# Hybrid decoder step on one core: where the last block's down weights are loaded and split, and when the last two attention heads' merge weights are formed

## The chip, the cores and the metric

One core of a Trainium2 chip runs the whole step as one program. The metric is device time in microseconds (us): the median of three runs, and beside it one profiled execution, whose rows are the ones read here. The core has five engines with a queue each: PE (TensorE, with its weight loads shown as PEld), ACT (ScalarE), DVE (VectorE), POOL (GpSimd) and SP, which here only issues transfers. An engine takes its instructions strictly in program order (the kernel fixes that order itself), so an instruction that waits holds up all behind it on the same engine.

## What is computed

One layer for 2048 prompt positions and 32 sample rows (8 sequences of 4), model width 1024, all in float32:

```
z = rmsnorm(x, g) @ w_in                     # q | k | v | u | gate
o, lse = three dilated attention branches    # 8 heads of 64; (128,1) (512,4) (2048,16)
att = sum_b softmax_b(lse_b) * o_b           # per position and head
x = x + concat(att, u * gate(v)) @ w_out
h = rmsnorm(x, g2)
x = x + (silu(h @ w_gate) * (h @ w_up)) @ w_down     # hidden width 2816
y = rmsnorm(x, final_g)
```

The outputs are y for prompt and sample, the key and value windows, and the sample rows of the gate.

## The kernel before

Every float32 product is made of two rounded halves ("high" and "low") and three matmuls: high·high, high·low, low·high. The halves come from `split_sb` (L132): ACT rounds (L135), POOL subtracts (L138).

**Attention** is a list of items, 20 for each of the 8 heads, one item to a step. Work is entered in a plan with `at(step, phase, fn)`, and written out sorted by step and, in a step, by the phase order `early, exp, low, scores, turn, mid, values, out, misc, store`. One item's scores are made in its step (PE L856, or L935 for the strided branch), its bias in the next (DVE L862 or L940), its exponential in the one after that (ACT L867 or L950), its transposes after that (PE L883 or L959), its values later (PE L911, L971). When a head is done, `Stats` (L987) forms the weights that merge its branches, in six parts entered by `stats_of` (L1142): `a` multiplies the collected maxima and sums by a mask (POOL L997, or DVE for the last head's second half), `b` is two small matmuls on it (PE L1003), `c` takes differences (DVE L1010 to L1013), `weights_e` exponentials (ACT L1016), `weights_b` the normalised weights (DVE L1021 to L1025), `store` writes them to DRAM (SP L1031). `merge_load` reads them back (SP L1045), `merge` applies them (L1054, L1056, L1058, on POOL or DVE), `merge_store` writes the merged head (SP L1063). Between the last head's steps ACT and POOL also split the first rows of w_out (tile v, loaded by SP L1313), and SP loads merged heads (L1350).

**The feed-forward part** runs in three blocks of tokens; the last one has four tiles of 128 prompt rows and the sample rows. A block goes through 22 slices f of the hidden width. For a slice, `one(u, q)` is called for q = 0 to 6: `product` (L1596) makes 12 matmuls (L1606 to L1608, 272 columns wide in the last block) from weights that ACT rounded (`high`, L1545) and POOL completed (`low_half`, L1549) during the slice before; then `prepare` (L1570) does the low half q-1 and the high half q of slice f+1 and loads piece q of slice f+2 (SP L1504, 256 KB); then perhaps one 512 KB piece of the sample cache is copied through (`roll`, SP L1258, at q = 1 and 3 in the last block); then the down weights. ACT also makes the silu (L1646, at q = 2 and 5) and the rounded hidden values (L1656, after q = 6); DVE makes their low halves (L1274).

The down weights of a slice are 512 KB. There is one raw buffer, fd: `load_down` (SP L1588) fills it and can only start when the split of the slice before has been read out; `split_down` makes the two halves (tile dw, ACT L135 and POOL L138). The down products (`down_unit`, L1679) are done for two slices at a time: at an even f, behind products 3, 4 and 5, for slices f-2 and f-1: two tiles of 24 matmuls, then two more, then the sample rows (8 matmuls). Each group of six takes three matmuls on the even slice's dw and hidden values, then three on the odd slice's. The last two slices are done after the loop by `first_downs` (L1683) and `last_rows` (L1728).

"e" is an even slice below, "o" the odd one behind it, and "o+1" the even one behind that, in which their down products run.

Of the kernel before, what the change touches and what calls it, by code (L numbers as in the profile page):

```python
# [28 lines left out]
NF = FF // P  # L29
# [13 lines left out]
class Plan:  # L43
# [8 lines left out]
    def at(self, step, phase, fn, *args):  # L52
        self.events.append((step, self.PHASES.index(phase), self.n, fn, args))
        self.n += 1
# [10 lines left out]
def hymba_step(ctx: ExitStack, tc: tile.TileContext, A: dict, O: dict):  # L65
    nc = tc.nc
    sync, act, dve, pool, pe = nc.sync, nc.scalar, nc.vector, nc.gpsimd, nc.tensor
# [7 lines left out]
    turn = [0, 0, 0, 0]  # L75
# [56 lines left out]
    def split_sb(hi, lo, src, eng_hi=None, eng_lo=None):  # L132

        if eng_hi is None:
            act.activation(hi, src, AF.Copy)  # L135
        else:
            eng_hi.tensor_copy(hi, src)
        (eng_lo or pool).tensor_sub(lo, src, hi.bitcast(F32))  # L138
# [22 lines left out]
    at = plan.at  # L161
# [517 lines left out]
    for half in range(2):  # L679
        for ki, kind in enumerate(ORDER[half]):  # L680
            for gi, tiles in enumerate(GROUPS):
# [13 lines left out]
                for j, tj in enumerate(tiles):  # L695
                    t = half * 8 + tj
                    e, ph = e0 + 2 * j, "out"
                    if last:
                        e, ph = e0, "early"
                    elif third:  # L700

                        e, ph = (e0 + 2 * j + 2, "out") if j < 2 else (e0, "early")
# [18 lines left out]
                    else:  # L721
                        layer_norm(e + 1, t, lambda t=t: zn["g", t], P, lambda t=t: gate_tile(t))

                        f = e + 4 + ((3 if half else 5) if tj in (4, 5) else 0)
# [417 lines left out]
    def stats_of(h, steps, r0, r1):  # L1142
        d = {}
        at(*steps[0], lambda: d.update(s=Stats(h, sts[h], r0, r1, dve if r0 else pool)))
        for (y, ph), fn in zip(steps, "a b c weights_e weights_b store".split()):
            at(y, ph, lambda fn=fn: getattr(d["s"], fn)())

    for h in range(H):

        s0 = B0 + (h + 1) * NI  # L1150
        end = h == H - 1
        ahead = h == H - 2
        if end:

            x = s0 - NI
            stats_of(h, [(x + y, ph) for y, ph in ((14, "early"), (14, "turn"), (15, "early"), (16, "early"), (16, "early"), (16, "mid"))], 0, 64)
            steps = ((2, "early"), (2, "turn"), (3, "early"), (4, "early"), (5, "early"), (5, "early"))
            at(x + 18, "mid", merge_load, h, 0)
            for part in range(3):
                at(x + 20 + part, "store", merge, h, 0, dve, part)  # L1160
                at(x + 21 + part, "store", merge, h, 1, pool, part)
            at(x + 24, "store", merge_store, h, 0, 2)
        else:
            steps = ((2, "misc"), (3, "misc"), (4, "early"), (5, "early"), (5, "misc"), (6, "mid"))

            for ch, (a, b) in enumerate(((8, 11), (8, 14), (11, 17), (11, 24) if ahead else (11, 20))):
                if ch % 2 == 0:
                    at(s0 + a, "mid", merge_load, h, ch)
                for part in range(3):
                    at(s0 + b + part, "store", merge, h, ch, pool, part)  # L1170
            if ahead:
                at(s0 + 17, "store", merge_store, h, 0, 2)
                at(s0 + 27, "store", merge_store, h, 2, 4)
            else:
                at(s0 + 23, "store", merge_store, h, 0, 4)
        stats_of(h, [(s0 + y, ph) for y, ph in steps], 64 if end else 0, P)
    for i, it in enumerate(items):
        x, h, n = B0 + i, it["h"], it["n"]
# [66 lines left out]
    def ob_pair(name):  # L1245
        t_ = lo.tile([P, 2, 1024], F32R, name=name, tag="ob", bufs=2)
        return t_[:, 0], t_[:, 1]
# [338 lines left out]
    def load_down(f):  # L1586
        raws["d", f] = w_ = pool_["fd"]
        sync.dma_start(w_, A["w_down"][f * P:(f + 1) * P, :])  # L1588
# [3 lines left out]
    def split_down(f):  # L1592
        wd[f % FC] = ob_pair("dw")
        split_sb(*wd[f % FC], raws.pop(("d", f)))
# [207 lines left out]
    B = blocks[0]  # L1802
# [55 lines left out]
    h = H - 1  # L1858
# [51 lines left out]
    def first_block(B):  # L1910

        m2, m1 = acc_place(2), acc_place(4)
        split_early(B, 1, m1)
        split_early(B, 2, m2)
        B.place()
        load_cat(B, 0, KD - 1, KD)
        load_cat(B, 5, 0, KD)
        merge_load(h, 2)
        load_acc(B, 1)
        load_acc(B, 0)  # L1920
        half1_load(*range(KD))
        sync.dma_start(gain[0], dap(A["final_g"], 0, [[0, P], [1, D]]))
        plan.run(10 ** 9)
        split_early(B, 3)
        for n, what in ((2, [(merge, h, 2, pool), (merge, h, 3, pool), (split_cat, B, 0), (split_early, B, 4)]),
                        (4, [(merge_store, h, 2, 4)]), (5, [(open_end, B, 1)]),
                        (6, [(half1_split, B, 0, 1)]), (7, [(open_end, B, 0), (split_cat, B, 5)]),
                        (8, [(half1_split, B, 2, 3)]), (9, [(half1_split, B, 4, 5), (sources, B, 0, 0, 1, 2, 3)]),
                        (10, [(half1_split, B, 6, 7)]), (11, [(sources, B, 1, 0, 1, 2, 3)])):
            later(n, both, *what)  # L1930
        for i in (1, 2, 3):
            open_unit(B, i)
        open_part(B, 0, (KD - 1,), False, True)
        for i in (4, 5):
            open_unit(B, i)
        first_operands(B)

        p2 = second_unit(B, 2)
        for i in (2, 3):
            load_acc(B, i)  # L1940
        second_end(B, 0, second_unit(B, 0))
        open_end(B, 2)
        second_end(B, 2, p2, 3)
        p1 = second_unit(B, 1)
        for i in (4, 5):
            load_acc(B, i)
        second_end(B, 1, p1)
        p3 = second_unit(B, 3)
        open_end(B, 3)
        second_end(B, 3, p3)  # L1950
        for i in (4, 5):
            open_end(B, i)
        for i in (4, 5):
            second_end(B, i, second_unit(B, i), 1)
# [54 lines left out]
    for bi, B in enumerate(blocks):  # L2009
        if bi == 0:  # L2010
            first_block(B)
        else:
            next_block(B, downs, finals)
        if B.last:
            hs4 = consts.tile([P, 4, 2 * SR], F32R, name="hs4", tag="cats")
        nb = None if B.last else blocks[bi + 1]

        part = 4
        units = [dict(f=f, a=0, b=B.nt) for f in range(NF)]
        if not B.last:  # L2020
            units[0:1] = [dict(f=0, a=0, b=part), dict(f=0, a=part, b=B.nt)]
        rows = list(range(len(B.rows)))
        last_h = {}

        def one(u, q):
            tick()
            product(B, u, q)
            f = u["f"]
            if u["b"] < B.nt:
                if bi == 0 and q in (0, 2):  # L2030
                    sources(B, 2, q, q + 1)
                return

            if f and q < 2:
                prepare(B, f, 7 + q)
            if f + 1 < NF:
                prepare(B, f + 1, q)
            if f + 2 < NF:
                if bi == 0 and f:
                    if q in (0, 2):  # L2040
                        sources(B, f + 2, q, q + 1)
                if bi == 0:
                    ahead_of(f + 2, q)
            elif nb:

                for s in {(0, 2): (0, 1), (0, 4): (2, 3), (1, 3): (4, 5), (1, 5): (6, 7)}.get((f + 2 - NF, q), ()):
                    load_wo(0, s, fraw)
                if f + 1 == NF and q > 0:
                    split_wo(nb, 0, q - 1, lambda s: op_tile())
            if f + 1 < NF and q in (1, 3, 5)[:(1, 3, 2)[bi]]:  # L2050
                roll(1)

            if q == 2 and f:
                load_down(f)
            elif q == (5 if f % 2 else 6):
                split_down(f)

        def downs_of(pair, a, b):
            for i in rows[a:b]:
                down_unit(B, i, pair)  # L2060

        for n, u in enumerate(units):
            u["n"] = n
            for q in range(7):
                one(u, q)
                if u["f"] % 2 == 0 and u["f"] > 0 and 3 <= q < 6:
                    downs_of((B.h[0], B.h[1]), *((0, 2), (2, 4), (4, 9))[q - 3])
        pair = (B.h[0], B.h[1])
        if B.last:
            last_rows(B, pair)  # L2070
        else:

            last = ([4] if nb.last else []) + [i for i in rows if not (nb.last and i == 4)]
            downs = [lambda B=B, pair=pair: first_downs(B, last[0], last[1], pair)]
            downs += [lambda B=B, pair=pair, i=i: down_unit(B, i, pair) for i in last[2:]]
            finals = [lambda B=B, nb=nb, i=i: final_a(B, i, (load_acc, nb, i) if i < len(nb.rows) else None) for i in last]
# [104 lines left out]
```

## Time and profile before

| | us |
|---|---|
| median of three runs | 2521.73 (2508.28, 2521.73, 2523.93) |
| profiled execution, its own time | 2527.26 |
| its span, first to last instruction | 2525.4 |
| PE busy in the span | 2442.6 (97%) |
| POOL, DVE, ACT busy | 1303.2, 1270.2, 1130.9 |
| mean granted TensorE clock | 0.989 |

A row of the timeline has start, length, engine, line, operation, output and inputs, and in brackets the idle time before it and who ended it. A row of the windows view has, for each engine, busy time and number of instructions in a stretch, then the granted clock and the transfers' share. SPq rows are transfers at their issue.

### The profile page before, as it was taken

The numbers are of one execution on the slowest core, as the hardware profiler recorded it, in microseconds if no ns is written. First come the engines' busy times: TensorE is split into PE (matmuls) and PEld (weight loads), VectorE is DVE, ScalarE is ACT, GpSimd is POOL, SyncE is SP. The second block draws the span as 40 slices with busy tenths as digits, with TensorE's granted clock in tenths as the row PEclk, the third lists the DMA queues.
The fourth block names the chain that finished last, engine by engine and source line by source line (L and its number), as shares of the span: only waits on it lengthen the run. The fifth ranks groups of instructions, "written<-read, shape, count | busy, mean of one in ns | idle before, by whom it ended". The sixth has DMA issues, their size and how long they took to land.

```text
span 2525.4 us, 39104 instructions
## 1 busy us (share of the span) xinstructions
PE 2442.6 (97%) x14022; PEld 2116.0 (84%) x14022; DVE 1270.2 (50%) x2595; ACT 1130.9 (45%) x2449; POOL 1303.2 (52%) x1019
## 2 busy tenths in 40 slices
PE   8998999999999899999999999999999998999997
PEld 7877776668887678999999989999999978888986
DVE  4558582217776645444444465444444465444444
ACT  7324343226666556454554446233233255333334
POOL 2216441005778447676776626445355445556565
PEclk9999999999999899999999999999999999999999
DMA  9974845675554554555555363535445363555553
GB/s 294 280 230 148 259 127 175 200 253 175 182 168 131 142 191 154 167 175 179 155 194 166 128 218 134 188 136 199 170 169 203 117 223 126 175 200 178 197 174 132
DMA packets 292292, 455.36 MB, mean 180 GB/s; under 512 B 28711, under 2 KB 160984, under 8 KB 286980
## 3 DMA queue, kind: packets, MB, share of 16 engines
q1 hardware_dynamic: 285252, 440.82, 53.6%
q10 hardware_dynamic: 6848, 12.06, 1.7%
q8 instruction: 111, 1.82, 0.3%
q14 instruction: 81, 0.66, 0.1%
HBM read 365.07 MB, written 157.84 MB: 207 GB/s over the span
## 4 chain that ended last, share of the span: by engine, by line
PE 62%; POOL 6%; issue 6%; DVE 3%; DMA 3%; ACT 2%; SPq 0%; POOLq 0%; DVEq 0%; ACTq 0%
PE ps_o L1679 15%; PE ps_m L1608 9%; PE ps_m L1607 9%; PE ps_m L1606 9%; POOL op L1549 4%; PE ps_s L856 3%; PE ps_o L911 2%; PE ps_t L883 1%; PE ps_s L935 1%; PE ps_s L318 1%; PE ps_o L1373 1%; PE ps_o L1375 1%; PE ps_o L1374 1%; PE ps_m L1373 1%; PE ps_m L1375 1%
## 5 line engine op out<-in xcount | busy, mean ns | idle before, releaser
L1549 POOL TENSOR_TENSOR op<-fr,op 128x512 fp32r<-128x512 f32 x385 | 487.5, 1299 | 246.6 <-ACT op L1545 232.5
L1606 PE MATMUL ps_m<-xh,op 128*128 128x384 f32 (+3 forms) x1904 | 604.9, 318 | 0.7 <-DVE zn L1627 0.4
L1608 PE MATMUL ps_m<-xh,op 128*128 128x384 f32 (+3 forms) x1904 | 604.4, 317 | 0.0
L1607 PE MATMUL ps_m<-xl,op 128*128 128x384 f32 (+3 forms) x1904 | 603.9, 317 | 0.1
L1679 PE MATMUL ps_o<-dw,hw 128*128 128x512 f32 x2040 | 492.6, 396 | 20.4 <-POOL dw L138 12.6
L1679 PEld LDWEIGHTS ps_o<-dw,hw 128*128 128x128 f32 x2040 | 385.1, 190 | 106.3 <-POOL dw L138 16.5
L1606 PEld LDWEIGHTS ps_m<-xh,op 128*128 128x128 f32 x1904 | 360.2, 189 | 5.3 <-ACT xh L1450 0.7
L1607 PEld LDWEIGHTS ps_m<-xl,op 128*128 128x128 f32 x1904 | 360.0, 189 | 4.0 <-DVE xl L1462 0.4
L1681 DVE TENSOR_TENSOR acc<-acc,ps_o 128x512 f32<-128x512 f32 (+1 forms) x362 | 248.3, 687 | 226.8 <-PE ps_o L1679 226.8
L1608 PEld LDWEIGHTS ps_m<-xh,op 128*128 128x128 f32 x1904 | 359.9, 189 | 0.0
L1646 ACT ACTIVATE ps_t<-zn 128x384 f32<-128x384 f32 (+1 forms) x126 | 58.5, 465 | 500.7 <-DVE zn L1629 423.8
L138 POOL TENSOR_TENSOR dw<-fd,dw 128x1024 fp32r<-128x1024 f32 x66 | 158.5, 2401 | 204.2 <-ACT dw L135 194.0
L1545 ACT ACTIVATE op<-fr 128x512 fp32r<-128x512 f32 x396 | 233.8, 626 | 3.4 <-PE ps_m L1375 3.4
L318 PE MATMUL ps_s<-wh,xh 128*128 128x512 f32 x480 | 196.8, 410 | 6.0 <-ACT xh L135 6.0
L320 PE MATMUL ps_s<-wh,xl 128*128 128x512 f32 x480 | 189.0, 394 | 0.0
L319 PE MATMUL ps_s<-wl,xh 128*128 128x512 f32 x480 | 188.9, 394 | 0.0
L1549 POOL TENSOR_TENSOR op<-pair,op 128x512 fp32r<-128x512 f32 x63 | 81.3, 1298 | 113.7 <-ACT op L1545 109.3
L536 POOL TENSOR_TENSOR pr<-kv,qb 96x512 f32<-96x512 f32 x32 | 45.6, 1425 | 170.3 <-DMA kv<-in_cache_k_dram 86.1
L318 PEld LDWEIGHTS ps_s<-wh,xh 128*128 128x128 f32 x480 | 90.9, 189 | 48.5 <-issue 23.7
L1656 ACT ACTIVATE hw<-ps_t 128x384 fp32r<-128x384 f32 (+1 forms) x126 | 54.2, 449 | 157.7 <-DVE ps_t L1652 157.7
L927 POOL CAST sq<-k 128x512 fp32r<-128x512 f32 x32 | 34.1, 1066 | 164.8 <-PE ps_s L319 164.8
L1274 DVE TENSOR_TENSOR hw<-ps_t,hw 128x384 fp32r<-128x384 f32 (+1 forms) x120 | 59.3, 508 | 109.7 <-ACT hs L1660 57.0
(490 smaller groups left out, 4328.7 us busy)
## 6 DMA issues: line engine op xcount, KB each, us to landing
fr<-ab_d SPq DMA_DIRECT2D x308, 256.0 KB
fd<-in_w_down_dram SPq DMA_DIRECT2D x66, 512.0 KB
out_ks_dram<-in_cache_k_dram SPq DMA_DIRECT2D x56, 512.0 KB
out_vs_dram<-in_cache_v_dram SPq DMA_DIRECT2D x56, 512.0 KB
ab_d<-fr SPq DMA_DIRECT2D x88, 256.0 KB
qk_d<-pair SPq DMA_DIRECT2D x64, 256.0 KB
ab_d<-pair SPq DMA_DIRECT2D x63, 256.0 KB
kv<-in_cache_k_dram SPq DMA_DIRECT2D x64, 192.0 KB
```

The source lines that it names most:

```text
L138: (eng_lo or pool).tensor_sub(lo, src, hi.bitcast(F32))
L318: pe.matmul(o[j], xh[:, k, :], wh, start=(k == 0), stop=False)
L319: pe.matmul(o[j], xh[:, k, :], wl, start=False, stop=False)
L320: pe.matmul(o[j], xl[:, k, :], wh, start=False, stop=(k == KD - 1))
L856: pe.matmul(s[:, a:b_], d[q][:, qs], d["k"][:, t0:t0 + b_ - a], start=(z == 0), stop=(z == 1))
L1545: act.activation(ops[f, j][0], ab[f][j], AF.Copy)
L1549: (pool if f or j in POOL_LOW else dve).tensor_sub(lo_, ab[f][j], hi.bitcast(F32))
L1606: pe.matmul(out, wh[:, ks], xh[:, :, k], start=(k == 0), stop=False)
L1607: pe.matmul(out, wh[:, ks], xl[:, :, k], start=False, stop=False)
L1608: pe.matmul(out, wl[:, ks], xh[:, :, k], start=False, stop=(k == 3))
L1679: pe.matmul(ps[0:nr], l_, r_[:, cs], start=(z == 0 and y == 0), stop=(z == FC - 1 and y == len(pairs) - 1))
L1681: dve.tensor_add(B.acc[i][0:nr, cs], B.acc[i][0:nr, cs], ps[0:nr])
```

## The change

Two things. In the last block, `split_down(f)` of an odd slice is called at q = 3 and not at q = 5, and `load_down(f + 1)` is called directly behind every split, where before `load_down(f)` stood at q = 2 of its own slice. In the other blocks nothing moves. In the attention, for the next to last head and the first half of the last one, the parts `b` to `store` of the merge weights are entered one step later (part `a` stays), and DVE's three parts of the last head's first merge one step later too.

```diff
-            stats_of(h, [(x + y, ph) for y, ph in ((14, "early"), (14, "turn"), (15, "early"), (16, "early"), (16, "early"), (16, "mid"))], 0, 64)
+            stats_of(h, [(x + y, ph) for y, ph in ((14, "early"), (15, "turn"), (16, "early"), (16, "early"), (17, "early"), (17, "mid"))], 0, 64)
...
-                at(x + 20 + part, "store", merge, h, 0, dve, part)
+                at(x + 21 + part, "store", merge, h, 0, dve, part)
...
-            steps = ((2, "misc"), (3, "misc"), (4, "early"), (5, "early"), (5, "misc"), (6, "mid"))
+            steps = (((2, "misc"), (4, "misc"), (5, "early"), (6, "early"), (6, "misc"), (7, "mid")) if ahead else
+                     ((2, "misc"), (3, "misc"), (4, "early"), (5, "early"), (5, "misc"), (6, "mid")))
...
-            if q == 2 and f:
+            if B.last:
+                if q == (3 if f % 2 else 6):
+                    split_down(f)
+                    if f + 1 < NF:
+                        load_down(f + 1)
+            elif q == 2 and f:
                 load_down(f)
             elif q == (5 if f % 2 else 6):
                 split_down(f)
```

(`ahead` is true for the next to last head.) In the changed program the lines from L1165 to L2052 carry a number one higher, so L1504 is L1505 there.

SP in the last block, one odd slice and the start of the even one (out<-in of each transfer; fr are pieces of the next slices' weights, out_vs the cache copies). Before:

```order
994 L1504 DMA fr<-ab_d 128x512
995 L1588 DMA fd<-in_w_down_dram 128x1024
996 L1504 DMA fr<-ab_d 128x512
997 L1258 DMA out_vs_dram<-in_cache_v_dram 16x8192
998 L1504 DMA fr<-ab_d 128x512 x5
999 L1258 DMA out_vs_dram<-in_cache_v_dram 16x8192
1000 L1504 DMA fr<-ab_d 128x512
```

and now:

```order
1002 L1505 DMA fr<-ab_d 128x512 x3
1003 L1589 DMA fd<-in_w_down_dram 128x1024
1004 L1505 DMA fr<-ab_d 128x512 x2
1005 L1259 DMA out_vs_dram<-in_cache_v_dram 16x8192
1006 L1505 DMA fr<-ab_d 128x512 x2
1007 L1259 DMA out_vs_dram<-in_cache_v_dram 16x8064
1008 L1589 DMA fd<-in_w_down_dram 128x1024
```

The odd slice's fd has moved ahead of two fr pieces, a cache copy and a third fr piece; the even slice's stands behind the cache copy of q = 3.

ACT around the split of an odd slice (op is a high half, the first L1646 the silu of q = 2, the second that of q = 5, hw and hs the hidden values). Before:

```order
1744 L1646 ACTIVATE ps_t_23656<-zn 128x272
1745 L1545 ACTIVATE op<-fr 128x512 x3
1746 L1646 ACTIVATE ps_t_23720<-zn 128x272
1747 L1545 ACTIVATE op<-fr 128x512
1748 L135 ACTIVATE dw<-fd 128x1024
1749 L1656 ACTIVATE hw<-ps_t_23720 128x4x64
```

and now:

```order
1751 L1647 ACTIVATE ps_t_23657<-zn 128x272
1752 L1546 ACTIVATE op<-fr 128x512 x2
1753 L135 ACTIVATE dw<-fd 128x1024
1754 L1546 ACTIVATE op<-fr 128x512
1755 L1647 ACTIVATE ps_t_23724<-zn 128x272
1756 L1546 ACTIVATE op<-fr 128x512
1757 L1657 ACTIVATE hw<-ps_t_23724 128x4x64
```

The split has moved ahead of two high halves and the second silu. On POOL it moves likewise: between the even and the odd split stand four low halves where six stood, and behind the odd split ten where eight stood.

PE in the last head, around the first half's two small matmuls (ps_o and ps_t with a number are banks of PSUM). Before:

```order
3062 L856 MATMUL ps_s<-k,ql 128x256
3063 L1003 MATMUL ps_o_8785<-sel_r,sm 64x16 x2
3064 L883 MATMUL ps_t_8788<-ident,e 128x128 x3
3065 L883 MATMUL ps_t_8793<-ident,e 128x128 x2
3066 L971 MATMUL ps_o_8796<-eT,v 64x64 x8
```

and now:

```order
3062 L856 MATMUL ps_s<-k,ql 128x256
3063 L883 MATMUL ps_o_8785<-ident,e 128x128 x3
3064 L883 MATMUL ps_t_8790<-ident,e 128x128 x2
3065 L971 MATMUL ps_o_8793<-eT,v 64x64 x8
3066 L856 MATMUL ps_s<-k,qh 128x384
3067 L856 MATMUL ps_s<-k,qh 128x256
3068 L856 MATMUL ps_s<-k,ql 128x384
3069 L856 MATMUL ps_s<-k,ql 128x256
3070 L1003 MATMUL ps_t_8817<-sel_r,sm 64x16 x2
```

The two matmuls have moved behind the transposes and strided values of their own step and the scores of the next. On DVE the parts `c` and `weights_b` each move behind one more pair of L894 (a transposed piece) and L862 (a bias). For the next to last head the two matmuls move behind only two score matmuls.

## The prediction

> **What bounds the kernel now.** First the page's busy times: PE works nearly all the time, so only what leaves PE standing or slows it can be gained.
>
> ```profile
> PE 2442.6 (97%) x14022; PEld 2116.0 (84%) x14022; DVE 1270.2 (50%) x2595; ACT 1130.9 (45%) x2449; POOL 1303.2 (52%) x1019
> ```
>
> Then the waits of PE in the stretch of the last block, and the first tile pair of each of its ten groups of down products, in the windows view (L1679 only; granted clock third from the right, of 1.00):
>
> ```profile
> PE ps_o L1679 <- POOL dw L138: 11.6, 10, 1.3
> PE ps_o L1679 <- ACT hw L1656: 4.5, 6, 1.2
> ...
> 2137.80:2149.10 11.30, 8.84 (x24) 6.28 (x24) 0.70 0.54 168
> 2177.50:2187.00 9.50, 7.63 (x24) 5.41 (x24) 0.82 0.56 176
> ...
> 2287.20:2296.40 9.20, 7.63 (x24) 5.43 (x24) 0.81 0.55 171
> 2324.80:2334.90 10.10, 7.55 (x24) 5.42 (x24) 0.83 0.56 169
> 2363.30:2369.60 6.30, 5.75 (x24) 4.29 (x24) 1.00 0.38 113
> ...
> sum 83.70, PE 67.10 PEld 48.27; mean PE 6.71 PEld 4.83
> ```
>
> The second pair of a group is the same 24 matmuls and waits for nothing:
>
> ```profile
> 2297.93 5.63 PE L1679 MATMUL ps_o<-dw,hw 128*128 128x512 f32 x24
> 2303.40 0.29 PE L1606 MATMUL ps_m<-xh,op 128*128 128x272 f32 x1
> ```
>
> It takes 2303.40 - 2297.93 = 5.47, 0.228 a matmul. Ten take 54.7; the first pairs take 83.7, from which 0.5 goes off because the stretches' edges are rounded outward. **So 28.5 us are lost there**, more than the 16.1 that the waits add up to. Four pairs ran at a lowered clock: 11.3 x 0.30 + 9.5 x 0.18 + 9.2 x 0.19 + 10.1 x 0.17 = 8.6. The other 19.9 is waiting, part of it hidden by modelled ends.
>
> One group shows why. Rows of PE, SP, ACT and POOL in turn:
>
> ```profile
> 2269.07 0.29 PE L1606 MATMUL ps_m<-xh,op 128*128 128x272 f32 x1
> 2285.72 0.29 PE L1606 MATMUL ps_m<-xh,op 128*128 128x272 f32 x1
> ...
> 2287.22 0.86 PE L1679 MATMUL ps_o<-dw,hw 128*128 128x512 f32 x3
> 2288.28 0.49 PE L1679 MATMUL ps_o<-dw,hw 128*128 128x512 f32 x1 [0.20 <-ACT hw L1656]
> 2290.12 6.45 PE L1679 MATMUL ps_o<-dw,hw 128*128 128x512 f32 x20 [1.35 <-POOL dw L138]
> ...
> 2279.03 0.52 SPq L1258 DMA_DIRECT2D out_vs_dram<-in_cache_v_dram  x1
> 2280.28 0.42 SPq L1588 DMA_DIRECT2D fd<-in_w_down_dram  x1
> ...
> 2272.59 1.06 ACT L135 ACTIVATE dw<-fd 128x1024 fp32r<-128x1024 f32 x1
> 2276.14 1.66 ACT L1545 ACTIVATE op<-fr 128x512 fp32r<-128x512 f32 x3
> 2286.55 1.06 ACT L135 ACTIVATE dw<-fd 128x1024 fp32r<-128x1024 f32 x1 [5.27 <-DMA fd<-in_w_down_dram]
> ...
> 2273.73 2.40 POOL L138 TENSOR_TENSOR dw<-fd,dw 128x1024 fp32r<-128x1024 f32 x1 [3.48 <-ACT dw L135]
> 2276.08 7.53 POOL L1549 TENSOR_TENSOR op<-fr,op 128x512 fp32r<-128x512 f32 x6
> 2287.69 2.38 POOL L138 TENSOR_TENSOR dw<-fd,dw 128x1024 fp32r<-128x1024 f32 x1 [4.07 <-ACT dw L135]
> ```
>
> PE starts product 6 of e at 2269.07 and is at product 3 of o+1 at 2285.72: eleven products in 16.65, 1.51 each. The odd fd is issued at 2280.28, 1.25 behind a cache copy of the same size, and lands at 2286.55, 6.3 later. ACT has stood 5.27 for it, with hw queued behind; POOL's low half begins at 2287.69, and the fifth matmul of the group, which reads it, at 2290.12 instead of 2287.22 + 4 x 0.228 = 2288.13.
>
> **Down weights, part by part.** Nothing is added: the same 21 loads and 22 splits, in other places.
>
> The load. fd is free when POOL has done the even split, 2273.73 + 2.40 = 2276.13. SP is then at this load; the next fr waits for POOL's next low half (2276.08 + 1.26) anyway, so no transfer behind it is held up. Issue: 2276.2, 4.1 earlier. How long it takes on a quiet queue the last slice shows, whose load found nothing before it:
>
> ```profile
> 2494.50 0.34 SPq L1588 DMA_DIRECT2D fd<-in_w_down_dram  x1
> 2498.66 0.40 ACT L1646 ACTIVATE ps_t<-zn 128x272 f32<-128x272 f32 x1 [4.12 <-DVE zn L1629]
> 2499.00 1.04 ACT L135 ACTIVATE dw<-fd 128x1024 fp32r<-128x1024 f32 x1
> ```
>
> ACT went from the silu into the split without a gap: at most 4.5. Behind a cache copy it took up to 7.2:
>
> ```profile
> 2317.92 0.43 SPq L1588 DMA_DIRECT2D fd<-in_w_down_dram  x1
> 2325.16 1.06 ACT L135 ACTIVATE dw<-fd 128x1024 fp32r<-128x1024 f32 x1 [6.23 <-DMA fd<-in_w_down_dram]
> ```
>
> Bounds for the landing are thus 4.5 and 7.2. I take 4.5: in the new order the copies of q = 1 stand behind the load.
>
> ACT. At q = 3 it has done two of three high halves, at 2276.14 + 1.11 = 2277.25, and waits for the landing at 2280.7; the split ends at 2281.8. Queued behind are a high half (1.66 / 3 = 0.55), the silu of q = 5 and hw: silu to 2282.7, DVE's product of it 0.45 (row below), hw and a second round by about 2284.4. PE wants hw of o as its fourth matmul, 2287.91. So 3.5 us cover it; DVE, which waits for the silu, holds a PSUM bank that PE needs at 2285.72, with 2 us to spare.
>
> ```profile
> 2280.76 0.45 DVE L1652 TENSOR_TENSOR ps_t<-ps_t,raw 128x272 f32<-128x272 f32 x1 [0.47 <-ACT ps_t L1646]
> ```
>
> POOL. Four low halves from 2276.08 end at 2281.1; the split runs from 2281.8 to 2284.2; **the next low half, that of q = 3, ends at 2285.45**. PE reads it as third matmul of product 3, at 2285.72 + 0.25 = 2285.97. Here is the thin cover, 0.5 us: a landing later than 5.0 makes PE wait here, microsecond for microsecond. The down products, from 2287.2, find both halves of dw done.
>
> The even load, issued near 2284.2 for a split near 2310, has some 25 us, and SP's fr pieces behind it wait for low halves that POOL does later still. In the last pair the load waits for the split of slice 20 as before; ACT now stands at q = 3 for it and makes the silu behind the split, some 1.4 later (one split, and a landing up to 0.3 behind where the silu was); the first twelve matmuls of the end, 12 x 0.228 = 2.7, still cover hw, barely. **Term: -28.5** (between -28.5 and, at 7.2, about +10; worked out under the rivals).
>
> What lowers the clock matters. LDWEIGHTS of L1679 shows two speeds, and each of the four lowered pairs holds waits of 2 us or less and no other cause that I see:
>
> ```profile
> L1679 PEld LDWEIGHTS ps_o<-dw,hw x2040: 186/188/334, 998.7 to 2513.8; 128*128 128x128 f32 x186
> ```
>
> The Trainium skill ("TensorE: Matmul & The Clock Gate", Part 1: The HAM clock gate) has the clock fall to half after an idle window of about 3.4 us. The near half speed agrees; the idle length does not, since no wait here is as long.
>
> **Merge weights.** Three places, rows of PE, ACT, DVE:
>
> ```profile
> 820.43 0.62 PE L1003 MATMUL ps_o<-sel_r,sm 128*128 128x16 f32 x4 [2.07 <-POOL sm L997]
> 843.77 0.61 PE L1003 MATMUL ps_o<-sel_r,sm 128*64 128x16 f32 x4 [2.19 <-POOL sm L997]
> 849.71 0.69 PE L911 MATMUL ps_o<-pt,v 128*64 128x256 f32 x2 [0.58 <-ACT o L981]
> 856.10 0.56 PE L856 MATMUL ps_s<-k,qh 128*128 128x384 f32 x2 [2.12 <-DVE st L862]
> 868.66 0.59 PE L1003 MATMUL ps_t<-sel_r,sm 128*128 128x16 f32 x4 [1.86 <-DVE sm L997]
> ...
> 848.75 0.63 ACT L135 ACTIVATE op<-v 128x512 fp32r<-128x512 f32 x1 [3.01 <-DMA v<-in_w_out_dram]
> ...
> 851.51 1.24 DVE L1021 TENSOR_TENSOR dd<-f,s 64x16 f32<-64x16 f32 x1 [4.67 <-ACT f L1016]
> 866.70 0.94 DVE L1056 TENSOR_TENSOR o<-o,raw 128x256 f32<-128x256 f32 x1
> ...
> 840.00:850.00 10.00, 7.24 (x58) 5.89 (x58) 2.97 (x12) 4.24 (x11) 4.18 (x6) 0.69 1.00 241
> ```
>
> At 820 the small matmuls pass two score matmuls (about 0.6); at 843.77 the wait of 2.19 is filled with transposes, values and scores. But PE's next stop, 849.71, waits for ACT, and ACT for a w_out piece until 848.75, with the transfers 1.00 busy. PE came to the wait at 843.77 - 2.19 = 841.58; the work behind it took 849.13 - 844.38 = 4.75, much of it at the lowered clock, and is now done by 846.3 or sooner. So PE only stands longer at 849.71, 3.4 or more: both gains are lost at this point. Behind it DVE's wait of 4.67 has one bias less queued, so the 2.12 at 856.10 can go; against it, the longer stand can cost a lowered stretch, up to 10 x (1 - 0.69) = 3.1. At 868.66 DVE's L997 now runs ahead of L1056: -0.8. The next to last head's weights, formed behind one more DVE pass (such as L1056's 0.9), can delay the transfers that PE meets at 849.71, since SP takes them in order. Bounds: -0.8 - 2.1 = -2.9 and 3.1 + 0.9 - 0.8 = +3.2. **Term: -1.0**, the certain 0.8 and a little of the 2.12.
>
> **Sum.** 2527.3 - 28.5 - 1.0 = 2497.8 against the profiled execution's own time. That execution is 5.5 above the median; if its lowered stretches are part of that, the gain at the median is up to 5.5 smaller. From 2521.7 this gives 2492.2 to 2497.7; I take 2495.0. A measurement of this kernel tells about 1% from no change, 25.2 us: below 2496.5 is faster.
>
> **The rivals.**
> (a) *POOL's low half takes the place.* The load still takes about 5.7, since fr pieces crowd it: 0.7 of wait in each of ten groups at product 3, and lowered stretches stay (8.6). Gain 28.5 + 1.0 - 7 - 8.6 = 14: 2508. For it: only 0.5 us of cover. Against: nothing is issued for 5.9 us before the load.
> (b) *The same place, slower.* At 7.2 each group waits 2.2 and draws a lowered stretch (8.6 / 4 = 2.15): 10 x 4.35 = 43.5 against 28.5, so +15, less 1: 2536. It decides from a landing of about 5.0 + 0.7 = 5.7 with such stretches, or 7.9 without. Against it: the same row order as in (a).
> (c) *The clock is not lowered by these waits* but by something that stays. Then 8.6 stays: 2495 + 8.6 = 2503.6. For it: six pairs with like waits kept 1.00. Against: the quoted second pair, the same matmuls without waits, ran at full speed. The Trainium skill's rule on idle windows, named above, would speak for this one.
> (d) *The change does not do what it says:* the load cannot leave earlier because fd is read until later. The rows give fd free at 2276.13, so only if POOL were behind. 2521.
>
> **How the numbers follow.** Forecast 0.70, (a) 0.12, (b) 0.05, (c) 0.09, (d) 0.04. The forecast's own spread, 2488 to 2501 from the merge term and the median, lies for about 0.7 of it below 2496.5: 0.49, and (a) and (c) add 0.01. Faster by over 1% 0.50, within 1% 0.46, slower 0.04, most of (b). Range 2486 to 2513: it takes in (a) and (c) and leaves out (b) and (d).
>
> **What would show it.** Right: in the last block L1679's waits for dw and hw gone, each first pair at 5.47, clock 1.00 there; ACT waiting 3 to 4 us for fd at q = 3, load to split start under 5 us; L1608 without waits for POOL. Wrong: L1608 waiting for POOL op L1549, or load times above 5.7. In the attention: no PE wait at 843, a longer one at 849, L1003's last wait about 1 us.

## The result and the profile after

| | before | after |
|---|---|---|
| median (lowest to highest), us | 2521.73 (2508.28 to 2524.78, 5 runs) | 2497.71 (2491.31 to 2498.77, 5 runs) |
| profiled execution, its own time | 2527.26 | 2497.73 |
| its span | 2525.4 | 2495.9 |
| granted clock, mean | 0.989 | 0.992 |

The ratio is 0.9898, with a 95% interval from 0.9867 to 0.9929: 24 us, or 1.0%, faster. The profiled executions differ by 29.5, more than the medians; where the other 5 come from is told below.

The page's busy times after, then all waits of PE in the stretch of the last block (2060 to the end):

```profile
PE 2430.9 (97%) x14022; PEld 2111.4 (85%) x14022; DVE 1273.4 (51%) x2595; ACT 1131.7 (45%) x2449; POOL 1305.1 (52%) x1019
```

```profile
PE ps_t L1440 <- ACT pair L1493: 3.5, 1, 3.5
PE ps_o L1680 <- DVE acc L1682: 1.5, 1, 1.5
PE ps_t L1440 <- ACT xns L1427: 1.1, 1, 1.1
PE ps_m L1607 <- ACT xh L1451: 0.5, 1, 0.5
```

No wait of the down products (L1680) for dw or hw is left, and none of the products (L1607 to L1609) for POOL has come. PE has as many matmuls as before and is busy 11.7 less: matmuls at a lowered clock, and the modelled ends of waiting ones, count as busy. The first tile pairs of the down products, in the windows view (L1680 only; clock third from the right):

```profile
2136.80:2142.40 5.60, 5.55 (x24) 4.37 (x24) 1.00 0.92 320
...
2442.30:2447.90 5.60, 5.53 (x24) 4.39 (x24) 1.00 0.94 330
sum 55.90, PE 55.42 PEld 43.68; mean PE 5.54 PEld 4.37
```

Each of the ten takes 5.49 from its first matmul to the product behind it, and has the full clock. By the same measure they took 83.2 before and 54.9 now: **28.3 us of the 29.5 come from here**.

One group after, SP, ACT, POOL and PE in turn:

```profile
2261.57 0.33 SPq L1589 DMA_DIRECT2D fd<-in_w_down_dram  x1
...
2265.03 1.06 ACT L135 ACTIVATE dw<-fd 128x1024 fp32r<-128x1024 f32 x1 [2.34 <-DMA fd<-in_w_down_dram]
...
2259.15 2.40 POOL L138 TENSOR_TENSOR dw<-fd,dw 128x1024 fp32r<-128x1024 f32 x1 [3.48 <-ACT dw L135]
2261.50 5.04 POOL L1550 TENSOR_TENSOR op<-fr,op 128x512 fp32r<-128x512 f32 x4
2266.48 2.42 POOL L138 TENSOR_TENSOR dw<-fd,dw 128x1024 fp32r<-128x1024 f32 x1
2268.83 5.08 POOL L1550 TENSOR_TENSOR op<-fr,op 128x512 fp32r<-128x512 f32 x4
...
2272.63 5.65 PE L1680 MATMUL ps_o<-dw,hw 128*128 128x512 f32 x24
```

The load leaves as POOL ends the even split (2259.15 + 2.40 = 2261.55), and ACT starts the odd split 3.46 later. POOL has both low halves of dw done at 2268.9, 3.7 before the down products begin. The low half of q = 3 is done at 2268.83 + 5.08 / 4 = 2270.10; PE reads it as third matmul of a product that begins 1.51 before the group, at 2271.37: 1.3 us of cover.

In the attention, rows of PE, one of ACT, and the windows view around the wait:

```profile
822.57 0.62 PE L1003 MATMUL ps_o<-sel_r,sm 128*128 128x16 f32 x4 [1.56 <-POOL sm L997]
845.26 0.41 PE L1003 MATMUL ps_t<-sel_r,sm 128*64 128x16 f32 x4 [0.28 <-POOL sm L997]
851.24 2.40 PE L911 MATMUL ps_o<-pt,v 128*64 128x256 f32 x12 [4.88 <-ACT o L981]
867.85 0.59 PE L1003 MATMUL ps_t<-sel_r,sm 128*128 128x16 f32 x4 [0.80 <-DVE sm L997]
...
850.29 0.63 ACT L135 ACTIVATE op<-v 128x512 fp32r<-128x512 f32 x1 [5.98 <-DMA v<-in_w_out_dram]
...
840.00:850.00 10.00, 6.08 (x67) 4.91 (x65) 5.16 (x16) 4.31 (x11) 5.13 (x6) 0.99 1.08 261
850.00:860.00 10.00, 8.76 (x51) 6.60 (x51) 4.68 (x10) 6.89 (x17) 6.37 (x7) 0.67 0.50 135
```

The wait at the two small matmuls has gone from 2.19 to 0.28, and PE stands at L911 instead, 4.88 where it stood 0.58, because ACT waits 5.98 for a piece of w_out. The lowered clock has moved from the stretch 840 to 850 to the one behind the wait.

### The profile page after: what moved, and what is told of

Read it like the earlier page. It is cut to its first block, busy times and chain, and to the rows that moved or that the text cites. A ratio compares the mean times of both kernels' runs of the same rounds, so it can differ in the third digit from the quotient of the medians.

```text
span 2495.9 us, 39114 instructions
## 1 busy us (share of the span) xinstructions
PE 2430.9 (97%) x14022; PEld 2111.4 (85%) x14022; DVE 1273.4 (51%) x2595; ACT 1131.7 (45%) x2449; POOL 1305.1 (52%) x1019
## 4 chain that ended last, share of the span: by engine, by line
PE 72%; DVE 3%; POOL 2%; ACT 2%; issue 1%; DMA 1%; SPq 1%; DVEq 0%; ACTq 0%; POOLq 0%
PE ps_o L1680 19%; PE ps_m L1609 11%; PE ps_m L1607 11%; PE ps_m L1608 11%; PE ps_s L856 2%; PE ps_o L911 2%; PE ps_t L883 1%; PE ps_s L935 1%; PE ps_s L318 1%; PE ps_o L1374 1%; PE ps_o L1376 1%; PE ps_o L1375 1%; PE ps_m L1374 1%; PE ps_m L1376 1%; PE ps_m L1375 1%
## 5 line engine op out<-in xcount | busy, mean ns | idle before, releaser
L1607 PE MATMUL ps_m<-xh,op 128*128 128x384 f32 (+3 forms) x1904 | 604.9, 318 | 0.9 <-ACT xh L1451 0.5
L1609 PE MATMUL ps_m<-xh,op 128*128 128x384 f32 (+3 forms) x1904 | 604.5, 317 | 0.0
L1680 PE MATMUL ps_o<-dw,hw 128*128 128x512 f32 x2040 | 480.4, 391 | 4.1 <-DVE acc L1682 3.3
L1680 PEld LDWEIGHTS ps_o<-dw,hw 128*128 128x128 f32 x2040 | 380.4, 188 | 82.6 <-DVE acc L1682 5.0
L1607 PEld LDWEIGHTS ps_m<-xh,op 128*128 128x128 f32 x1904 | 360.3, 189 | 5.3 <-ACT xh L1451 0.7
L1609 PEld LDWEIGHTS ps_m<-xh,op 128*128 128x128 f32 x1904 | 360.0, 189 | 0.0
L1518 ACT ACTIVATE fr<-fr,g2c 128x128 f32<-128x128 f32 x352 | 108.3, 387 | 0.0
```

The source lines that it names most:

```text
L1518: act.activation(w_[:, k * P:(k + 1) * P], w_[:, k * P:(k + 1) * P], AF.Copy, scale=g2c[:, kk:kk + 1])
L1607: pe.matmul(out, wh[:, ks], xh[:, :, k], start=(k == 0), stop=False)
L1609: pe.matmul(out, wl[:, ks], xh[:, :, k], start=False, stop=(k == 3))
L1680: pe.matmul(ps[0:nr], l_, r_[:, cs], start=(z == 0 and y == 0), stop=(z == FC - 1 and y == len(pairs) - 1))
```

## The experiments

The theory: the odd down load stood too late in SP's order, and its landing set the down products; the early load is the whole gain, the split's earlier place and the merge weights count for little. The rivals: the split's place carries it; the merge weights carry a part; and, from the prediction, a late landing moves the wait to POOL's low half. Diffs are against the changed kernel.

**Each part alone.** First the down weights without the merge weights:

```diff
-            stats_of(h, [(x + y, ph) for y, ph in ((14, "early"), (15, "turn"), (16, "early"), (16, "early"), (17, "early"), (17, "mid"))], 0, 64)
+            stats_of(h, [(x + y, ph) for y, ph in ((14, "early"), (14, "turn"), (15, "early"), (16, "early"), (16, "early"), (16, "mid"))], 0, 64)
...
-                at(x + 21 + part, "store", merge, h, 0, dve, part)
+                at(x + 20 + part, "store", merge, h, 0, dve, part)
...
-            steps = (((2, "misc"), (4, "misc"), (5, "early"), (6, "early"), (6, "misc"), (7, "mid")) if ahead else
-                     ((2, "misc"), (3, "misc"), (4, "early"), (5, "early"), (5, "misc"), (6, "mid")))
+            steps = ((2, "misc"), (3, "misc"), (4, "early"), (5, "early"), (5, "misc"), (6, "mid"))
```

> The last block's half of the change alone; the merge weights stand where they stood before. My theory: almost the whole gain is here, 28 us: each first pair of down products at 5.5 us, granted clock 1.00 in all ten, and a median of about 2495 to 2500. In the attention PE waits 2.2 us at the small matmuls of the last head again. Rival (the merge weights carry a good part of the gain): the median stays above 2503. Rival (the clock is lowered by something else than these waits): some of the ten pairs still run at 0.70 to 0.83.

Then the merge weights without the down weights:

```diff
-            if B.last:
-                if q == (3 if f % 2 else 6):
-                    split_down(f)
-                    if f + 1 < NF:
-                        load_down(f + 1)
-            elif q == 2 and f:
+            if q == 2 and f:
```

> The merge weights' half of the change alone; the down weights are loaded and split as before. My theory: 1 to 3 us faster than before, not told from no change by its time: about 2519 to 2521. In the trace the wait of 2.2 us at the last head's first small matmuls is gone, a wait of about 5 us for ACT stands some 6 us later, and the stretch behind it is shorter. The first pairs of down products still take 6 to 11 us. Rival: 8 us or more faster, 2513 or less.

Measured, beside 2524.05 of the kernel before: down weights alone 2499.24 (ratio 0.9911, 0.9887 to 0.9935), merge weights alone 2521.93 (1.0001, 0.9981 to 1.0021). The first has every first pair at 5.49, as the changed kernel; the second waits as before:

```profile
PE ps_o L1680 <- POOL dw L138: 11.0, 10, 1.3
```

The down weights are the whole of what can be measured. For the merge weights alone I had expected 1 to 3 us in the median, and nothing shows, although their signs are in the trace: the wait at the first small matmuls is down to 0.26, and PE stands 6.32 for ACT at L911. The second run's ten first pairs take 74.1 where the profiled execution of before took 83.2, since only two of them, and not four, had a lowered clock, and only two, not six, waited for hw as well as for dw:

```profile
2137.50:2147.00 9.50, 0.82 0.60 186
2175.30:2182.10 6.80, 1.00 0.38 119
...
2423.60:2433.10 9.50, 0.82 0.55 178
```

So in one and the same order of the last block the loss is 28.5 in one execution and 74.1 - 54.9 = 19.2 in another. The two executions' own times, 2527.26 and 2517.88, differ by 9.4, and their ten pairs by 9.1. This is why the medians differ by 24 to 25 and the first pair of profiles by 29.5.

**Load or split.** The early load with the split at its old place:

```diff
-                if q == (3 if f % 2 else 6):
+                if q == (5 if f % 2 else 6):
                     split_down(f)
```

> The changed kernel, but the odd slices are split at q = 5 again, as before; only the load moves, directly behind the former split. My theory (the late landing was the whole cause): as fast as the changed kernel, within 3 us of it, first pairs at 5.5 us; ACT does not wait for the load at all or less than 1 us, and POOL's low halves of q = 3 and 4 are ready some 3 us sooner than in the changed kernel. Rival (the split's earlier place is needed as well): first pairs of 6.5 us and more, 10 us or more slower than the changed kernel.

And the early split with the load at its old place:

```diff
             if B.last:
-                if q == (3 if f % 2 else 6):
+                if q == 2 and f:
+                    load_down(f)
+                elif q == (3 if f % 2 else 6):
                     split_down(f)
-                    if f + 1 < NF:
-                        load_down(f + 1)
```

> The changed kernel, but the load stands at q = 2 of its own slice again; only the odd split moves, to q = 3. My theory: ACT stands at q = 3 until the load lands near where it landed before, POOL's split ends as late as before, and now a low half is behind it that PE needs at product 3 of the even slice: PE waits there 4 to 6 us in each of ten groups, with a lowered clock after it. Slower than before: about 10 x (5.5 + 2 - 2.85) = 46 us, 2555 to 2575. Rival (the split's place makes the gain, or POOL's low halves have more cover than I worked out): not slower than 2522.

Measured: 2499.59 (0.9915, 0.9886 to 0.9944) and 2569.65 (1.0199, 1.0164 to 1.0235). The early load alone gives the whole gain: ACT comes to the split 5.0 after the load's issue and does not wait at all. The stretch from the end of PE's wait near 935, behind the attention, to the end of the span tells it more sharply: it takes 1589.3 in the profiled execution of before, 1580.4 with the merge weights alone, and 1560.7 in the changed kernel, with the down weights alone and with the early load alone. The early split alone is 45.6 us slower than the kernel before. Its waits of PE in the last block and one split on ACT:

```profile
PE ps_m L1607 <- ACT hs L1661: 25.8, 8, 4.1
PE ps_m L1609 <- POOL op L1550: 11.8, 10, 1.5
...
PE ps_m L1607 <- DVE zn L1636: 3.1, 1, 3.1
PE ps_m L1607 <- DVE raw L1636: 2.7, 1, 2.7
...
2257.30 1.06 ACT L135 ACTIVATE dw<-fd 128x1024 fp32r<-128x1024 f32 x1 [8.76 <-DMA fd<-in_w_down_dram]
```

ACT stands 8.76 for the load with the silu of q = 5 queued behind; DVE waits for the silu with a PSUM bank in hand, and the first matmul of a product (L1607) waits for the bank: 31.6 of the 43.4. In eight of the ten waits the view names ACT's hs. But that row ends as PE already runs (at 2260.14 in this group), and DVE's last reading of the bank (L1636) ends 0.13 to 0.15 before PE starts in all ten:

```profile
2259.55 0.42 DVE L1636 TENSOR_TENSOR raw<-raw,ps_m 128x272 f32<-128x272 f32 x1
...
2260.12 0.57 PE L1607 MATMUL ps_m<-xh,op 128*128 128x272 f32 x1 [2.98 <-ACT hs L1661]
```

POOL's low half, which the prediction took as the thin place, costs only 11.8. For a landing this late the bank is the first limit, not the low half. So the time lies in the range that I gave, and the waits of 4.3 in a group are in their 4 to 6, but for the larger part not at the place that I named.

**A crowded queue, first try.** Two copies of the cache are moved, so that three stand in SP's order directly ahead of the odd load, with the split at q = 3 and at q = 5:

```diff
-            if f + 1 < NF and q in (1, 3, 5)[:(1, 3, 2)[bi]]:
+            if B.last:
+                if f + 1 < NF and q == 6:
+                    roll(1 if f % 2 else 3)
+            elif f + 1 < NF and q in (1, 3, 5)[:(1, 3, 2)[bi]]:
                 roll(1)
```

> The changed kernel, but the last block's copies of the sample cache stand at q = 6, three at an even slice right ahead of the odd slice's load and one at an odd slice, instead of one each at q = 1 and 3: the same number of copies, with the load behind 1.5 MB of them. My theory (the cover is POOL's low half for product 3, which with a landing 3.5 us after the issue is ready 1.3 us early): the load lands 6 to 8 us after its issue, and PE waits at product 3 of the even slice and at the first products' banks behind DVE, 1 to 4 us in each group: 2512 to 2535. Rival (transfers pass each other, the load lands in 4 us all the same): within 3 us of the changed kernel.

> The same crowded copies, with the odd split at q = 5 as before, so that POOL's low halves of q = 3 and 4 go ahead of it. My theory: the split's own place has more cover, since the down products want dw only some 7 us behind the split's new place: waits of under 1 us in a group, 2497 to 2508, and at least 8 us faster than with the odd split at q = 3 under the same copies. Rival (the split's place does not matter): as slow as that one.

Measured, beside 2523.19: 2498.75 (0.9913, 0.9895 to 0.9931) and 2497.98 (0.9905, 0.9888 to 0.9922). The first is far below its range. The second is inside its own, but the 8 us by which it should have been faster than the first did not come. The rows of the first run (SP, ACT, then the transfers' share and GB/s, last two columns):

```profile
2253.67 1.78 SPq L1259 DMA_DIRECT2D out_vs_dram<-in_cache_v_dram  x3
2259.18 0.34 SPq L1589 DMA_DIRECT2D fd<-in_w_down_dram  x1
...
2262.68 1.06 ACT L135 ACTIVATE dw<-fd 128x1024 fp32r<-128x1024 f32 x1 [2.37 <-DMA fd<-in_w_down_dram]
...
2253.00:2256.00 3.00, 1.00 0.81 262
2256.00:2259.00 3.00, 1.00 0.88 350
2259.00:2262.70 3.70, 1.00 0.60 200
```

The experiment did not do what it was meant to. SP issues the copies and then waits 3.7 for POOL to free fd; in that time the copies run, and the load takes 3.50 in this group. In nine groups with this wait the loads take 3.50 to 4.85, on average 4.2 against 3.6 in the changed kernel: a little later, but no wait of PE comes of it. "Directly ahead" in the order was not directly ahead in the queue. One group did show the mechanism: in the block's first, the load came 2.65 behind the copies' issue and took 5.44, and PE waited 1.06 for POOL's low half in product 3.

**A crowded queue, second try.** Now the load's first 64 columns take the wait for fd, and one copy stands between them and the rest (that of q = 3 of the even slice is moved there):

```diff
-    def load_down(f):
+    def load_down(f, copies=0):
         raws["d", f] = w_ = pool_["fd"]
-        sync.dma_start(w_, A["w_down"][f * P:(f + 1) * P, :])
+        c = 64 if copies else 0
+        if copies:
+            sync.dma_start(w_[:, :c], A["w_down"][f * P:(f + 1) * P, :c])
+            roll(copies)
+        sync.dma_start(w_[:, c:], A["w_down"][f * P:(f + 1) * P, c:])
...
-            if f + 1 < NF and q in (1, 3, 5)[:(1, 3, 2)[bi]]:
+            if f + 1 < NF and q in (1, 3, 5)[:(1, 3, 2 if f % 2 else 1)[bi]]:
...
-                        load_down(f + 1)
+                        load_down(f + 1, 0 if f % 2 else 1)
```

> The changed kernel with the odd down load truly late: its first 64 columns go as a small transfer that takes the wait for the free buffer, then one 512 KB cache copy (moved here from q = 3 of the even slice), then the other 960 columns. In the changed kernel the landing is at most 3.5 us behind the end of POOL's even split and POOL's low half of q = 3 is ready 1.3 us ahead of product 3, so it may come up to about 4.8 behind it. Here the load is issued about 1.3 later and takes 5.0 to 7.2 behind the copy, so it lands 6.3 to 8.5 behind the split. Theory (late landing moves the wait to product 3 through POOL's low half): a wait of 1.5 to 3.7 in each of ten groups, some with a lowered clock behind it: 2513 to 2550, PE waiting at the third matmul row of product 3 for POOL. Rival (the queue has so much room that a copy directly ahead delays nothing): 2495 to 2501 and no such waits.

The same with the split at q = 5:

> As the run with the load behind a copy, but with the odd split back at q = 5. There POOL makes all low halves of the slice before the split, and the odd dw's low half is read only by the fifth matmul of the down group: with an early load that split ends 2.2 us ahead of it, and the split starts 5.0 behind POOL's even one. Theory: a landing 6.3 to 8.5 behind moves the split 1.3 to 3.5 later and leaves 0 to 1.3 of wait in each group, at the down products and not at product 3: 2498 to 2512, and at least 10 below the run with the split at q = 3. Rival (the place of the split makes no difference to a late load): the two runs within 5 us of each other.

Measured, beside 2523.56 of before and 2498.76 of the changed kernel in the same rounds: 2508.07 (0.9945, 0.9928 to 0.9963) and 2501.30 (0.9914, 0.9897 to 0.9932). Rows of the first (SP, ACT, POOL, PE; L1613 is the third matmul of a product here) and the waits of PE:

```profile
2266.17 0.33 SPq L1591 DMA_DIRECT2D fd<-in_w_down_dram  x1
2266.55 0.52 SPq L1259 DMA_DIRECT2D out_vs_dram<-in_cache_v_dram  x1
2267.12 0.57 SPq L1593 DMA_DIRECT2D fd<-in_w_down_dram  x1
...
2271.82 1.06 ACT L135 ACTIVATE dw<-fd 128x1024 fp32r<-128x1024 f32 x1 [4.53 <-DMA fd<-in_w_down_dram]
...
2276.66 0.39 PE L1613 MATMUL ps_m<-xh,op 128*128 128x272 f32 x1 [0.52 <-POOL op L1550]
```

```profile
PE ps_m L1613 <- POOL op L1550: 6.9, 10, 1.4
...
PE ps_o L1700 <- ACT hw L1661: 0.7, 1, 0.7
```

The landing came 5.65 after the first issue in this group, and in the ten 5.57 to 6.58, on average 5.76: less late than the 6.3 I took as the least, so the time fell short of its range. The place is the one expected: ten waits for POOL's low half in product 3 and none at the first pairs, which stay at 5.49 and full clock. From 5.76 less the mean wait of 0.7 follows a limit near 5.1. With the split at q = 5 these waits are gone (one of 1.3 for dw is left, in the last pair): 6.8 us apart, where I expected 10 or more, and 2501.30 is in its range. In the profiled executions, from 935 to the end, the two are 9.3 apart.

**The piece of w_out.** The last four splits of w_out on ACT one step later, with the split of the down weights at q = 3, then at q = 5:

```diff
-    for s, (a, b) in enumerate(((-12, -9), (-12, -9), (-12, -8), (-12, -7), (-8, -5), (-8, -4), (-7, -3), (-6, -2))):
+    for s, (a, b) in enumerate(((-12, -9), (-12, -9), (-12, -8), (-12, -7), (-8, -4), (-8, -3), (-7, -2), (-6, -1))):
```

> The changed kernel, with the last four splits of w_out in the last head one step later, so that ACT does not stand for a w_out piece ahead of the copy (L981) that PE waits for. My theory (the time that the merge weights' new place sets free is lost at this wait): the wait of about 5 us at PE's L911 goes; part of it, 2 to 3 us, comes back as time, 2494 to 2496. Rival (the next item's exponential, queued behind the same piece, stops PE as long): no gain, within 1 us of the changed kernel.

> The changed kernel with the odd split back at q = 5 (the load stays early) and the last four splits of w_out one step later. My theory: as the kernel with the later w_out splits alone, 2494 to 2496; the odd split's place adds nothing on a quiet queue. Rival: another 3 us or more either way.

Measured: 2499.89 (0.9913, 0.9898 to 0.9927) and 2497.56 (0.9907, 0.9893 to 0.9921), no gain: neither reached the expected 2494 to 2496. The wait at L911 is gone, but not the piece's lateness. Rows of PE and ACT of the first:

```profile
855.75 0.81 PE L883 MATMUL ps_t<-ident,e 128*128 128x128 f32 x5 [3.40 <-ACT e L867]
859.38 0.90 PE L856 MATMUL ps_s<-k,qh 128*128 128x384 f32 x2 [2.82 <-DVE st L862]
...
854.13 0.63 ACT L135 ACTIVATE op<-v 128x512 fp32r<-128x512 f32 x1 [6.06 <-DMA v<-in_w_out_dram]
```

ACT has done the attention's o and now stands 6.06 for the same transfer one step later, with the exponentials (L867) queued behind. 3.40 + 2.82 is not less than 4.88. What is late is the transfer.

**The size of the merge term.** The changed kernel and the one with the old merge weights once more, in the same rounds:

> The changed kernel once more, beside the next run, which is the same but for the merge weights, to see the size of the merge term on one chip and in the same rounds. Theory of the prediction: the later merge weights are worth about -1.0, so this run is 0.5 to 1.5 below the next. Rival: they are worth nothing that shows, the two within 0.5 or of the other sign.

> The changed kernel with the merge weights at their old steps. Theory: 0.5 to 1.5 above the run before it, 2498 to 2501. Rival: within 0.5 of it or below it.

Measured: 2498.76 (0.9905, 0.9886 to 0.9924) and 2497.10 (0.9899, 0.9880 to 0.9917): the other sign from the first two, 2497.71 and 2499.24. Over the profiled executions I took the time from the last small matmuls ahead of the moved ones (L1003 near 782) to PE's wait near 935, the same two instructions in each: with the old weights 154.5, 151.8 and 155.0, with the new ones 149.2 to 154.0 (the nine executions with w_out's splits in their place, mean 151.9 against 153.8). The means are in favour of the change, by less than executions of one order differ among themselves. The size of the term stays open, between 0 and about -2.

## Why the prediction was right, and where a size was off

Forecast and result agree: 2495.0 against 2497.71, in the range, and the sum of 2497.8 made against the profiled execution meets its 2497.73. That these two meet to 0.1 is partly luck: in the second execution the code ahead of the change took 2.1 us more, and the attention from there to the wait near 935 took 3.0 less.

**The loss of 28.5 in the down products** was the term, and it went as a whole (28.3). Its split into 19.9 of waits and 8.6 of lowered clock is that of one execution; another lost 19.2 in all. The prediction took up to 5.5 off for that and then only 2.8 of it; the same-round comparisons give 24.8 (down weights alone) and 24.5 (early load alone), so about 4 off would have been right.

**The load.** Issue at the end of POOL's even split: right, to 0.02. Its time was too long: 4.5 was an upper bound from a slice whose ACT came late, and the measured one is 3.46 (3.42 to 3.62 in all slices but one, which took 4.34). The Trainium skill ("DMA: Bandwidth & Descriptors", Anatomy of one DMA) fits a transfer at 2.0 us and its bytes over 436 GB/s, on POOL's path; by that 512 KB would take an estimated 3.2. This load, on SP's, came within 0.3 of it. The loads of before took 4.95 to 7.24 in the ten groups; the two that I quoted are a middle one and the longest. More stood ahead of them than the one copy that I named. SP's rows in that kernel, and the transfers' share behind them:

```profile
2278.66 0.32 SPq L1504 DMA_DIRECT2D fr<-ab_d  x1
2279.03 0.52 SPq L1258 DMA_DIRECT2D out_vs_dram<-in_cache_v_dram  x1
2279.90 0.33 SPq L1504 DMA_DIRECT2D fr<-ab_d  x1
2280.28 0.42 SPq L1588 DMA_DIRECT2D fd<-in_w_down_dram  x1
...
2280.00:2283.00 3.00, 1.00 0.87 299
2283.00:2287.00 4.00, 1.00 1.00 368
```

Two pieces and the copy, 1 MB, go out within 1.6 ahead of it, and the DMA engines are 0.87 to 1.00 busy until it lands. Behind one copy alone the rest of the load took 4.70 (2267.12 to 2271.82).

**ACT** waits at q = 3 as said, mostly 2.3 to 2.5 and at most 3.4, not 3 to 4, by the shorter landing. **POOL's low half as the thin cover**: the place is right, shown by ten waits there when the load was late; the cover is 1.3 and not 0.5, again the landing. The limit of 5.0 was right: 3.46 + 1.3 = 4.8 here, and 0.3 more because POOL, still busy, starts its split that much later than ACT's end would let it; about 5.1 with the late load. **DVE and the PSUM bank**, 2 us to spare, I named and then left out of rivals (a) and (b); with a landing after 8.76 of waiting it is the larger cost. So the price of rival (b), from low halves and clock alone, was too low for very late loads. **The last pair** is barely covered, as said: no wait in the changed kernel, 0.7 for hw with the late load.

**The merge weights.** The steps were right: the waits at 820 and 843 shrink by 0.51 and 1.91, the stand at L911 grows to 4.88 (3.4 or more, I said), the 2.12 at 856 is gone, and the last wait is 1.06 shorter (0.8, I said). But one execution with the old weights (the down weights alone) has a last wait of 0.92 too, so not all of this is the change. The sum of -1.0 is neither shown nor refuted.

**The rivals.** (a) did not come, but it exists: at 5.76 on average the load costs 2508.07 - 2498.76 = 9.3 in ten groups. I gave 2508 for about that landing; that the numbers meet is partly chance, since I counted 8.6 of lowered clock that the run does not have. (b) did not come: a wait of 0.4 to 1.4 in product 3 lowered no clock. (c) fell: with the waits gone all ten pairs run at 1.00, in the changed kernel and with the down weights alone. (d) fell with the load's issue.

On the clock the Trainium skill has two accounts. By Part 1 of "TensorE: Matmul & The Clock Gate" it falls after an idle window of about 3.4 us; its section "A second HAM failure mode: psum-queue depth-cycling" tells of a kernel in which frequent short stands between groups of matmuls make it swing. The traces here agree with the first in the length, but a window need not be idle as a whole. The lowered stretches in the ten groups of before start at 2140.82, 2181.78, 2291.00 and 2328.55, last 3.41 (the first 6.83), and lie whole multiples of 3.41 apart: 12, 32 and 11. Cut on that grid, two groups of before look as follows (busy time of PE, then the clock, third from the right); PE waits twice in each, 0.52 and 1.33 in the first, 0.70 and 1.33 in the second:

```profile
2178.36:2181.77 3.41, 1.56 (x7) 1.00 0.10 37
2181.77:2185.18 3.41, 3.41 (x10) 0.50 0.53 133
...
2250.04:2253.45 3.41, 2.02 (x11) 1.00 0.44 168
2253.45:2256.86 3.41, 2.77 (x12) 1.00 0.15 16
2256.86:2260.27 3.41, 3.41 (x22) 1.00 0.98 294
```

In the first group both waits fall into one stretch: PE stands 1.85 of it, and the next runs at half clock. In the second the grid parts them, 1.39 and 0.64, and the clock stays. So it is with the others. In before and with the merge weights alone, PE stands 1.55 to 2.32 in the six stretches that a lowering follows, and in the others at most 1.39, but for one of 1.60 that kept the clock; the limit by these rows, whose ends are modelled, is near 1.6. With the early split alone it stands 2.25 to 3.41, and all ten groups are lowered; with the late load and the split at q = 3 at most 1.42, and none is. This is also why four groups lost the clock in one execution and two in another: in before six groups held two waits, with the merge weights alone two, and no group with a single wait lost it. Of the six pairs that I counted for (c), since they kept the clock with like waits, four had a single wait.

## What to carry to other kernels

Where a transfer fills a single buffer, issue it directly behind the instruction that frees the buffer, and look at what stands ahead of it in the issuing engine's order: here a 4 us later place in a burst cost 25 us over ten rounds, and in the quiet place the transfer took 3.4 to 4.3 instead of 4.95 to 7.24. Put the consumer on an engine as late as its own readers allow: with the load early, the split's old place lost nothing and bore a late load better, and with the load late the early split was 45.6 slower than before. Before a wait is filled, look one stop further on: a wait that a late transfer sets only moves, as it did twice at the piece of w_out.

## What I had not expected of the hardware

Copies that stand ahead of a waiting load in the issuing order cost it little when the wait is long enough: three of 512 KB were issued 3.7 us ahead, and the loads took 4.2 on average against 3.6 without them; 2.65 behind their issue one took 5.44. The clock goes by fixed stretches of 3.41 us here: two waits of at most 1.35 us halved it for the next stretch where they fell into the same one, and not where the grid parted them. The code ahead of the change varies by more than the smaller edits here: the instruction near 782 starts between 779.8 and 785.6 in fourteen executions, though nothing ahead of it differs.
